# A hybrid decoder layer on one core: a third tile for the forms of x, later stores of the gated and merged blocks, a third fetched tile

## The chip, the cores and the metric

The kernel runs on one core of a Trainium2 chip, in one launch. The core has TensorE (matrix products; PE in the profile, with its weight loads as PEld), VectorE (DVE), ScalarE (ACT), GpSimd (POOL) and SyncE (SP). In this kernel SP issues most transfers between DRAM and the core's memory, GpSimd some, and both take them strictly in the order in which they are written. The metric is the device time of the core, in microseconds.

## The reference

The layer has 256 tokens and a width of 2048, in float32, with a tolerance that asks for more than single rounded products. Cut to what matters:

```python
h = _rmsnorm(x, pre_norm_g)
proj = jnp.einsum('bsd,de->bse', h, w_in)
(q_a, c_kv, k_rope, z_mla, c_in, b_gate, c_gate, z_conv,
 g_mla, g_conv) = jnp.split(proj, cuts, axis=-1)
...
attn = _causal_mla_attention(q_nope, q_rope, k_nope, k_rope, v)
attn = attn.reshape(b, s, MLA_WIDTH) * jax.nn.silu(z_mla)
y_mla = jnp.einsum('bse,ed->bsd', attn, w_o_mla)

u = c_gate * c_in
u_pad = jnp.pad(u, ((0, 0), (CONV_K - 1, 0), (0, 0)))
conv = sum(conv_w[k] * u_pad[:, k:k + s] for k in range(CONV_K))
y_conv = jnp.einsum('bse,ed->bsd', b_gate * conv * jax.nn.silu(z_conv), w_o_conv)

merged = jax.nn.sigmoid(g_mla) * y_mla + jax.nn.sigmoid(g_conv) * y_conv
out = jnp.einsum('bsd,de->bse', merged, w_out)
x = x + _rmsnorm(out, post_norm_g)
```

Latent attention (16 heads) and a short gated convolution run side by side on the normed input; each is projected back to 2048 channels, the two are weighted by sigmoid gates that are themselves products of the input, and one more projection follows.

## The kernel before

**Numbers in two parts.** Every float32 operand is split into a high and a low part of a narrower type, and TensorE forms three products (high by high, high by low, low by high). For a block of weights that arrived in a tile `raw`, ScalarE writes the high part `whi` and VectorE the low part `wlo` (`split_act`, L264 to L266). The weights of 1 MB each stream through three `raw` tiles, loaded by SP (L167): a load can go when VectorE has made the low part of the block three loads earlier, and when SP has got that far in its queue.

**Three stages.** The first, up to about 607 us, makes the attention's latents, heads and softmax and the channels of the convolution; its products are called `cv`, `z`, `qn`, `kn`, `sc` and others. The second, 607 to 965 us, makes the two sigmoid gates and the two projections back to 2048 channels. The third makes the output projection (`out`), the norm and the residual.

**Forms.** The gates are made by a scheme of fewer products: seven sums and differences of blocks of the input ("forms", named 11, 22, 12, 5, 6, 7 and 3) are prepared in the first stage, in four chunks. `make_forms` (L871) is a generator that is stepped beside the other work. Per chunk it loads the input into `x_area`, scales it, and makes for each form the high part on ScalarE (L902) and the low part on VectorE (L904, L906) in a tile `form`, of which there are two; SP stores it to `far_form` in DRAM (L909). So a form can be written only when the store of the form two earlier has landed. The sums 5, 6, 7 and 3 are made in four tiles `form_sum0` to `form_sum3`. A scheduler with a simulated timeline settles where the ScalarE and VectorE instructions of a form stand among those around them; transfers stay in program order.

**Sets and units.** In the second stage four sets s0 to s3 (`paired`, L1243) make the gates of one block c of 512 channels each; their weight sums come by loads into tiles `b` (L1251) and by transfers of GpSimd that add to what lies there (L1256). Between their steps stand units of plain products (`sq`): `at_both` by the attention's projection in s0 and s1, `cv_both` by the convolution's in s2 and s3; `turned_cv` loads bring the convolution's channels. The order is a list `seq` of units; a unit may have something put behind it by `later(n, fn)` (L1157), n units on, and the loads of weights are sorted in ahead of the units that need them.

**Gated and merged blocks.** A set has four gate tiles, a to d; the tile of `sd` in one set is that of `sa` in the next, and so on round. Each block of gate and projection, per c and per half t of the tokens, is multiplied in the gate's tile as soon as both are there. For the first branch `weigh` (L1216) does this, and `keep` has SP store the result in DRAM (L1148), one unit late. For the second branch `merge` (L1230) multiplies, adds the stored block, which GpSimd has fetched again (`fetch`, L1224, L1151) into one of two tiles `m`, transposes the sum into the gate's tile (L358) and has SP store it with four transfers to `far_m` (L366), one unit late; then it fetches the next. `turned_m` loads, two per pair of blocks and issued by GpSimd (L964), bring the transposed blocks back, and ScalarE and VectorE split them into `m_both` for the output products. `m_load[1]` is the loader of blocks 2 and 3; its first load was put behind the fourth unit of the last plain block, its second follows later.

Of the kernel before, what the change touches and what calls it, by code (L numbers as in the profile page):

```python
# [11 lines left out]
F32 = mybir.dt.float32  # L12
# [70 lines left out]
def tile_layer(ctx: ExitStack, tc: tile.TileContext, xw, w0, xb, x, pos, pvec, post_g, wc, wz, wcv, wkr, wqk, wqr, wv, cwr, wsq, xf, out):  # L83
# [210 lines left out]
    const.tile([P, LINE - 8 + 112 + P], F32, name="const_pad")  # L294
    cos_t = const.tile([P, S], F32, name="cos_t")
    sin_t = const.tile([P, S], F32, name="sin_t")
    r_x = const.tile([P, S], F32, name="r_x")
# [32 lines left out]
    qa = lp.tile([P, KR, 2 * S], F32R, name="qa")  # L330
    ckv = lp.tile([P, KR, 2 * S], F32R, name="ckv")
    kr = bp.tile([P, 2, S], F32R, name="kr")
    mask = bp.tile([P, 3 * P], F32, name="mask")
# [537 lines left out]
    def make_forms():  # L871

        kq = 2
        area = early_pool.tile([P, 2, kq, S], F32, name="x_area")
        sums_4 = [early_pool.tile([P, kq, P], F32, name=f"form_sum{i}") for i in range(4)]
        for c in range(KH // kq):
# [16 lines left out]
            a12, a22 = area[:, 1, :, :P], area[:, 1, :, P:]  # L893
            u, w, f7, f3 = (f[:, :, :] for f in sums_4)

# [3 lines left out]
            def part(n, src, sign=1.0):  # L899
                f = early_pool.tile([P, kq, 2, P], F32R, name=f"form{n}_{c}", tag="form", bufs=2)  # L900
                hi, lo = f[:, :, 0, :], f[:, :, 1, :]
                nc.scalar.activation(hi, src, AF.Copy, scale=sign)  # L902
                if sign == 1.0:
                    nc.vector.tensor_tensor(lo, src, hi.bitcast(F32), op=ALU.subtract)  # L904
                else:
                    nc.vector.scalar_tensor_tensor(lo, src, sign, hi.bitcast(F32), op0=ALU.mult, op1=ALU.subtract)  # L906
                w = kq * 2 * P
                return lambda: tc.keep_in_program_order(
                    nc.sync.dma_start(  # L909
                        out=far_form[n][:, c * w : (c + 1) * w], in_=f[:, :, :, :].rearrange("p k j c -> p (k j c)").bitcast(F32)  # L910
                    )
                )

            todo = (
                ("11", a11, 1.0, None), ("22", a22, 1.0, None), ("12", a12, 1.0, (u, a22, a21, ALU.subtract)),
                ("5", u, 1.0, (w, u, a11, ALU.add)), ("6", w, -1.0, (f7, a11, a21, ALU.subtract)),
                ("7", f7, 1.0, (f3, w, a12, ALU.subtract)), ("3", f3, 1.0, None),
            )
# [238 lines left out]
    def later(n, fn):  # L1157
        pending.setdefault(now[0] + n, []).append(fn)
# [57 lines left out]
    def weigh(nc_, t):  # L1216
        n, c = nc_
        g = gate_of[n, c, t]
        nc.vector.tensor_tensor(g[:, :], sums_of[n, c][t][:, :], g[:, :], op=ALU.mult)
        later(1, lambda: keep(("m", c, t), g))  # L1220

    fetched, wanted = {}, []

    def fetch():  # L1224
        if wanted:
            c, t = wanted.pop(0)
            fetched[c, t] = wide(f"m{c}_{t}", "y", 2)
            again(("m", c, t), fetched[c, t])

    def merge(nc_, t):  # L1230
# [5 lines left out]
        nc.vector.tensor_tensor(m[:, :], m[:, :], g[:, :], op=ALU.add)  # L1236
        go, _ = turned(m[:, :], g[:, :], 4, far_m[c][:, 512 * t : 512 * (t + 1)], nc.sync)
        later(1, go)
        later(1, fetch)
# [142 lines left out]

    for u, m in ((s3["V7"][1], 0), (v[3][3], 1)):
        also(u, m_load[m][0][0])
    also(s3["V4"][0], m_load[0][0][1])
    also(s3["V4"][1], m_load[0][1][1])

    def first_fetches(order):
        wanted.extend(order)
        fetch()  # L1390
        fetch()

# [66 lines left out]
    assert not wanted and not fetched  # L1459

    last_m = m_load[2][0]

# [199 lines left out]
```

## Time and profile before

| | |
|---|---|
| median of 3 runs | 1057.33 us |
| lowest, highest run | 1054.04, 1061.59 us |
| profiled execution | 1061.88 us |
| its span | 1059.6 us |
| TensorE, busy | 1019.5 us, 96% of the span |
| VectorE, busy | 803.5 us, 76% |
| ScalarE, busy | 591.8 us, 56% |
| GpSimd, busy | 167.8 us, 16% |
| mean transfer rate | 256 GB/s |
| mean granted clock of TensorE | 0.988 |

TensorE is the engine that sets the end: it runs almost without a break, so the place to look is each of its stops and what ended it. In a row of the timeline the first number is the start in us from the start of the span, the second the duration, and the bracket the idle time of that engine just before and what ended it. A row of the waits gives the total, how many times, and the longest. The granted clock is the share of full speed that TensorE was given; it is 1.00 nearly everywhere and 0.5 for some microseconds behind some of the stops.

### The profile page before, as it was taken

Reading aid. Unit: us, or ns where it says so; the run is one execution under the profiler, and the core shown is the slowest. Engines: PE = TensorE matmul, PEld = TensorE weight load, DVE = VectorE, ACT = ScalarE, POOL = GpSimd, SP = SyncE. Lnnn points to the kernel's source line nnn. Section 1 sums busy time; section 2 is a strip of 40 time slices with the busy share of each in tenths; the row PEclk is TensorE's granted clock in tenths of the full one; section 3 lists DMA queues with packets and bytes.
Section 4 is the critical chain, followed back from the end, with each engine's and each line's share of the span. In section 5 each row is a group of like instructions: output and inputs, shape, how many; then the busy total and the mean of one; then the engine's idle time right before and its main releaser. Section 6 shows DMA issues by size and latency. Waiting matters only on the chain.

```text
span 1059.6 us, 13048 instructions
## 1 busy us (share of the span) xinstructions
PE 1019.5 (96%) x4552; PEld 840.8 (79%) x4552; DVE 803.5 (76%) x1101; ACT 591.8 (56%) x854; POOL 167.8 (16%) x304
## 2 busy tenths in 40 slices
PE   9999999999999989999999987999998999899997
PEld 8887888887788878788888865888787788688886
DVE  7588878677797768766887696788787889586662
ACT  7666656555565555455564554564664664573551
POOL 4620421213211132112232220000000000100000
PEclk9999999999999999989999998999999999999999
DMA  9775877668775786847787899689679487956942
GB/s 368 272 236 225 288 245 262 219 205 286 228 279 203 211 271 240 293 168 240 235 298 282 307 319 373 262 302 261 236 255 355 159 292 187 284 210 242 366 186 79
DMA packets 58993, 271.02 MB, mean 256 GB/s; under 512 B 9104, under 2 KB 15888, under 8 KB 33584
## 3 DMA queue, kind: packets, MB, share of 16 engines
q1 hardware_dynamic: 45792, 226.94, 59.0%
q0 software_dynamic: 12848, 42.07, 15.0%
q10 hardware_dynamic: 288, 1.20, 0.3%
q8 instruction: 35, 0.57, 0.2%
q14 instruction: 30, 0.25, 0.1%
HBM read 241.88 MB, written 24.12 MB: 251 GB/s over the span
## 4 chain that ended last, share of the span: by engine, by line
PE 77%; DMA 11%; DVE 6%; ACT 3%; issue 1%; SPq 1%; DVEq 0%; ACTq 0%
PE cv L88 26%; PE sq L88 13%; PE out L88 8%; PE sX L88 7%; PE z L88 7%; DMA far_form<-form 6%; DMA raw<-wsq_dram 4%; PE sZ L88 3%; DVE wlo L266 2%; PE qa L88 2%; PE ckv L88 2%; PE sY L88 2%; ACT whi L265 2%; PE qn L88 1%; DMA x_area<-xf_dram 1%
## 5 line engine op out<-in xcount | busy, mean ns | idle before, releaser
L265 ACT ACTIVATE whi<-raw 128x1024 fp32r<-128x1024 f32 (+1 forms) x302 | 305.2, 1027 | 252.2 <-PE cv L88 86.1
L266 DVE TENSOR_TENSOR wlo<-raw,whi 128x1024 fp32r<-128x1024 f32 (+1 forms) x300 | 352.2, 1187 | 121.1 <-ACT whi L265 101.6
L88 PE MATMUL cv<-whi,x_both 128*128 128x512 f32 x1024 | 323.4, 392 | 8.1 <-ACT cv_f L811 4.9
L88 PEld LDWEIGHTS cv<-whi,x_both 128*128 128x128 f32 x1024 | 193.6, 189 | 50.6 <-ACT cv_f L811 6.2
L88 PE MATMUL cv<-wlo,x_both 128*128 128x512 f32 x512 | 200.6, 392 | 1.5 <-DVE wlo L266 1.5
L88 PEld LDWEIGHTS cv<-wlo,x_both 128*128 128x128 f32 x512 | 96.9, 189 | 21.2 <-DVE wlo L266 1.8
L266 DVE TENSOR_TENSOR slo_V<-b,shi_V 128x1024 fp32r<-128x1024 f32 x60 | 71.6, 1220 | 18.4 <-PE sq L88 11.7
L265 ACT ACTIVATE shi_V<-b 128x1024 fp32r<-128x1024 f32 x60 | 61.2, 1052 | 37.8 <-PE sq L88 26.9
L88 PE MATMUL z<-whi,x_both 128*128 128x512 f32 x256 | 79.9, 389 | 0.0
L88 PE MATMUL sq<-whi,cv_both 128*128 128x512 f32 x256 | 63.9, 404 | 7.7 <-ACT whi L265 7.7
L366 POOL DMA_DIRECT2D far<-via x64 | 35.4, 559 | 224.0 <-DVE via L358 222.5
L88 PE MATMUL sq<-whi,at_both 128*128 128x512 f32 x256 | 62.3, 396 | 7.8 <-ACT whi L265 7.8
L88 PEld LDWEIGHTS sq<-whi,cv_both 128*128 128x128 f32 x256 | 50.0, 197 | 19.3 <-ACT whi L265 8.7
L88 PEld LDWEIGHTS sq<-whi,at_both 128*128 128x128 f32 x256 | 48.9, 192 | 19.1 <-ACT whi L265 8.8
L88 PEld LDWEIGHTS z<-whi,x_both 128*128 128x128 f32 x256 | 48.1, 188 | 9.9
L88 PE MATMUL sX<-shi_V,form 128*128 128x512 f32 x192 | 47.8, 391 | 2.3 <-ACT sb L1300 2.3
L88 PE MATMUL z<-wlo,x_both 128*128 128x512 f32 x128 | 49.8, 389 | 0.0
L88 PE MATMUL out<-whi,m_both 128*128 128x512 f32 x208 | 49.4, 389 | 0.0
L88 PEld LDWEIGHTS out<-whi,m_both 128*128 128x128 f32 x208 | 39.0, 188 | 8.1
L88 PEld LDWEIGHTS sX<-shi_V,form 128*128 128x128 f32 x192 | 35.8, 188 | 10.9 <-ACT sb L1300 3.6
L1256 POOL DMA_DIRECT2D b<-wsq_dram x10 | 8.7, 894 | 186.1 <-ACT whi L265 125.1
L266 DVE TENSOR_TENSOR slo_Q<-b,shi_Q 128x1024 fp32r<-128x1024 f32 x28 | 33.4, 1220 | 4.7 <-PE sq L88 3.2
(301 smaller groups left out, 1560.4 us busy)
## 6 DMA issues: line engine op xcount, KB each, us to landing
raw<-wcv_dram SPq DMA_DIRECT2D x64, 1024.0 KB, 6.1
raw<-wsq_dram SPq DMA_DIRECT2D x48, 1024.0 KB, 6.8
b<-wsq_dram SPq DMA_DIRECT2D x26, 1024.0 KB, 5.2
raw<-wz_dram SPq DMA_DIRECT2D x16, 1024.0 KB, 4.8
b<-wsq_dram POOLq DMA_DIRECT2D x10, 1024.0 KB, 10.7
raw<-wqk_dram SPq DMA_DIRECT2D x8, 1024.0 KB, 7.7
far_form<-form SPq DMA_DIRECT2D x28, 256.0 KB, 7.7
form<-far_form SPq DMA_DIRECT2D x7, 1024.0 KB, 11.2
```

What stands on the lines that cost most here:

```text
L88: return tc.keep_in_program_order(nc.tensor.matmul(*a, **kw))
L265: a = nc.scalar.activation(hi, src, AF.Copy)
L266: b = nc.vector.tensor_tensor(lo, src, hi.bitcast(F32), op=ALU.subtract)
L366: tc.keep_in_program_order(queue.dma_start(out=f[i], in_=m))
L1256: tc.keep_in_program_order(nc.gpsimd.dma_start(out=dst[:, :], in_=wsq[n, c + b, k], accum_op=ALU.add))
```

## The change

Five things change. The forms have three tiles in place of two, and the sums 7 and 3 are written over those of 5 and 6, so two tiles of sums are gone; the rotary tables `cos_t` and `sin_t` move to another pool. `weigh` stores its gated block four units late, not one. `merge` stores the merged blocks of c = 0 and 1 four units late on SP, and those of c = 2 and 3 at once on GpSimd. There are three tiles `m` for fetched blocks, and up to three fetches are made at first. The first load of `m_load[1]` is issued behind the whole list of units.

```diff
--- before.py
+++ after.py
@@ -292,8 +292,6 @@
     for _ in range(8):
         matmul(idle[:, :P], one, one, start=True, stop=True)
     const.tile([P, LINE - 8 + 112 + P], F32, name="const_pad")
-    cos_t = const.tile([P, S], F32, name="cos_t")
-    sin_t = const.tile([P, S], F32, name="sin_t")
     r_x = const.tile([P, S], F32, name="r_x")
     r_both = const.tile([P, LINE], F32, name="r_both")
     nc.gpsimd.memset(r_both[:, :], 0.0)
@@ -329,6 +327,8 @@
     lp = lstack.enter_context(tc.tile_pool(name="lp", bufs=1, side="right"))
     qa = lp.tile([P, KR, 2 * S], F32R, name="qa")
     ckv = lp.tile([P, KR, 2 * S], F32R, name="ckv")
+    cos_t = bp.tile([P, S], F32, name="cos_t")
+    sin_t = bp.tile([P, S], F32, name="sin_t")
     kr = bp.tile([P, 2, S], F32R, name="kr")
     mask = bp.tile([P, 3 * P], F32, name="mask")
     nc.gpsimd.memset(mask[:, :], 0.0)
@@ -872,7 +872,7 @@
 
         kq = 2
         area = early_pool.tile([P, 2, kq, S], F32, name="x_area")
-        sums_4 = [early_pool.tile([P, kq, P], F32, name=f"form_sum{i}") for i in range(4)]
+        sums_2 = [early_pool.tile([P, kq, P], F32, name=f"form_sum{i}") for i in range(2)]
         for c in range(KH // kq):
             for i in range(2):
                 tc.keep_in_program_order(
@@ -891,13 +891,13 @@
             yield
             a11, a21 = area[:, 0, :, :P], area[:, 0, :, P:]
             a12, a22 = area[:, 1, :, :P], area[:, 1, :, P:]
-            u, w, f7, f3 = (f[:, :, :] for f in sums_4)
+            u, w = (f[:, :, :] for f in sums_2)
 
             def tt(o, a, b, op):
                 nc.vector.tensor_tensor(o, a, b, op=op)
 
             def part(n, src, sign=1.0):
-                f = early_pool.tile([P, kq, 2, P], F32R, name=f"form{n}_{c}", tag="form", bufs=2)
+                f = early_pool.tile([P, kq, 2, P], F32R, name=f"form{n}_{c}", tag="form", bufs=3)
                 hi, lo = f[:, :, 0, :], f[:, :, 1, :]
                 nc.scalar.activation(hi, src, AF.Copy, scale=sign)
                 if sign == 1.0:
@@ -913,8 +913,8 @@
 
             todo = (
                 ("11", a11, 1.0, None), ("22", a22, 1.0, None), ("12", a12, 1.0, (u, a22, a21, ALU.subtract)),
-                ("5", u, 1.0, (w, u, a11, ALU.add)), ("6", w, -1.0, (f7, a11, a21, ALU.subtract)),
-                ("7", f7, 1.0, (f3, w, a12, ALU.subtract)), ("3", f3, 1.0, None),
+                ("5", u, 1.0, (w, u, a11, ALU.add)), ("6", w, -1.0, (u, a11, a21, ALU.subtract)),
+                ("7", u, 1.0, (w, w, a12, ALU.subtract)), ("3", w, 1.0, None),
             )
             for n, src, sign, following in todo:
                 go = part(n, src, sign)
@@ -1217,14 +1217,14 @@
         n, c = nc_
         g = gate_of[n, c, t]
         nc.vector.tensor_tensor(g[:, :], sums_of[n, c][t][:, :], g[:, :], op=ALU.mult)
-        later(1, lambda: keep(("m", c, t), g))
+        later(4, lambda: keep(("m", c, t), g))
 
     fetched, wanted = {}, []
 
     def fetch():
         if wanted:
             c, t = wanted.pop(0)
-            fetched[c, t] = wide(f"m{c}_{t}", "y", 2)
+            fetched[c, t] = wide(f"m{c}_{t}", "y", 3)
             again(("m", c, t), fetched[c, t])
 
     def merge(nc_, t):
@@ -1234,8 +1234,8 @@
         g, m = gate_of[n, c, t], fetched.pop((c, t))
         nc.vector.tensor_tensor(g[:, :], sums_of[n, c][t][:, :], g[:, :], op=ALU.mult)
         nc.vector.tensor_tensor(m[:, :], m[:, :], g[:, :], op=ALU.add)
-        go, _ = turned(m[:, :], g[:, :], 4, far_m[c][:, 512 * t : 512 * (t + 1)], nc.sync)
-        later(1, go)
+        go, _ = turned(m[:, :], g[:, :], 4, far_m[c][:, 512 * t : 512 * (t + 1)], nc.gpsimd if c > 1 else nc.sync)
+        later(0 if c > 1 else 4, go)
         later(1, fetch)
 
     sums_of, gate_of = {}, {}
@@ -1380,15 +1380,14 @@
         old = u[3]
         u[3] = lambda: (old and old(), fn())
 
-    for u, m in ((s3["V7"][1], 0), (v[3][3], 1)):
-        also(u, m_load[m][0][0])
+    also(s3["V7"][1], m_load[0][0][0])
     also(s3["V4"][0], m_load[0][0][1])
     also(s3["V4"][1], m_load[0][1][1])
 
     def first_fetches(order):
         wanted.extend(order)
-        fetch()
-        fetch()
+        for _ in range(min(3, len(order))):
+            fetch()
 
     also(s2["V6"][1], lambda: first_fetches([(0, 1), (0, 0), (1, 0), (1, 1)]))
     also(s3["V6"][1], lambda: first_fetches([(2, 1), (2, 0)]))
@@ -1458,6 +1457,7 @@
 
     assert not wanted and not fetched
 
+    m_load[1][0][0]()
     last_m = m_load[2][0]
 
     def out_products(pss, w, kk, ts=range(NT)):
```

TensorE's order is the same in both kernels. In the other engines' queues these places matter below.

ScalarE, second chunk of the forms (`form5_1` is form 5 of chunk 1; `half` is a copy for a rope, `cv_f` an eviction of a product of the channels, `whi` a weight's high part). Before:

```order
L433 ACTIVATE half_2443<-qr3_2416 128x256 [waits PE_49]
L902 ACTIVATE form5_1_2602<-form_sum0_1014 128x2x128 [waits DMAHW1_49]
L811 ACTIVATE cv_f_112<-cv4_0_2277,r_both_99 128x512 [waits PE_49]
L265 ACTIVATE whi51_1024_2530<-raw51_2458 128x1024 [waits DVE_49,PE_49]
L265 ACTIVATE qr_2437<-f_2442 64x256 [waits DVE_49]
```

After:

```order
L433 ACTIVATE half_2441<-qr3_2414 128x256 [waits PE_49]
L902 ACTIVATE form6_1_2639<-form_sum1_1015 128x2x128 [waits DMAHW1_49]
L811 ACTIVATE cv_f_110<-cv4_0_2275,r_both_97 128x512 [waits PE_49]
L265 ACTIVATE whi51_1024_2528<-raw51_2456 128x1024 [waits DVE_49,PE_49]
L265 ACTIVATE qr_2435<-f_2440 64x256 [waits DVE_49]
```

At the same place stands the next form, 6 in place of 5, and it waits for the same transfer semaphore; every form of a chunk from the third on has moved up by one form's place in this way.

ScalarE, the end of the same chunk (`kn` is the high part of a head's key, `qn_hi` of its query). Before:

```order
L433 ACTIVATE half_2723<-kn3_1_2699 128x256 [waits PE_49,Activation_49]
L902 ACTIVATE form3_1_2895<-form_sum3_1017 128x2x128 [waits DMAHW1_49]
L265 ACTIVATE kn_2677<-f_2716 128x256 [waits DVE_49]
L265 ACTIVATE kn_2677<-f_2722 128x256 [waits DVE_49]
L265 ACTIVATE whi56_1024_2818<-raw56_2728 128x1024 [waits PE_49]
```

After:

```order
L265 ACTIVATE qn_hi_2673<-f_2690 128x256 [waits DVE_49]
L433 ACTIVATE half_2721<-kn3_1_2697 128x256 [waits PE_49,Activation_49]
L265 ACTIVATE kn_2675<-f_2714 128x256 [waits DVE_49]
L265 ACTIVATE kn_2675<-f_2720 128x256 [waits DVE_49]
L265 ACTIVATE whi56_1024_2816<-raw56_2726 128x1024 [waits PE_49]
```

Form 3, the last of the chunk, no longer stands ahead of `kn`; it has taken the place of form 7 earlier on.

SP, the transition from set s2 to s3 (`b` are loads of weights for the gates, `raw` the streamed weights, `far_m` the stores of merged blocks of `sd`, `sa`, `sb`, `sc`, four transfers each). Before:

```order
L1251 DMA b_1_0_7561<-wsq_dram 128x2048
L366 DMA far_m_648<-sd_7556 32x4x128 x4
L1251 DMA b_1_1_7601<-wsq_dram 128x2048
L167 DMA raw_7624<-wsq_dram 128x2048
L1251 DMA b_1_2_7626<-wsq_dram 128x2048
L1251 DMA b_1_3_7649<-wsq_dram 128x2048
L366 DMA far_m_648<-sa_7086 32x4x128 x4
L366 DMA far_m_649<-sb_7344 32x4x128 x4
L366 DMA far_m_649<-sc_7394 32x4x128 x4
L167 DMA raw_7728<-wsq_dram 128x2048
L167 DMA raw_7752<-wsq_dram 128x2048
```

After:

```order
L1251 DMA b_1_0_7561<-wsq_dram 128x2048
L1251 DMA b_1_1_7597<-wsq_dram 128x2048
L167 DMA raw_7620<-wsq_dram 128x2048
L1251 DMA b_1_2_7622<-wsq_dram 128x2048
L1251 DMA b_1_3_7645<-wsq_dram 128x2048
L366 DMA far_m_648<-sd_7556 32x4x128 x4
L167 DMA raw_7714<-wsq_dram 128x2048
L167 DMA raw_7738<-wsq_dram 128x2048
L366 DMA far_m_648<-sa_7078 32x4x128 x4
L366 DMA far_m_649<-sb_7342 32x4x128 x4
L366 DMA far_m_649<-sc_7394 32x4x128 x4
L167 DMA raw_7843<-wsq_dram 128x2048
```

The stores of `sd` have moved behind three loads of `b` and one of `raw`, and two loads of `raw` now stand ahead of the twelve stores of `sa`, `sb` and `sc`, where they stood behind them. In the transition from s1 to s2 both `turned_cv` loads, which stood behind the stores of gated blocks `sa`, `sb` and `sc`, likewise stand ahead of them, with a `raw` and two `b` loads in between.

## Prediction

> **What bounds the kernel now.** I read the page first, for the busy shares.
>
> ```profile
> span 1059.6 us, 13048 instructions
> PE 1019.5 (96%) x4552; PEld 840.8 (79%) x4552; DVE 803.5 (76%) x1101; ACT 591.8 (56%) x854; POOL 167.8 (16%) x304
> ```
>
> TensorE is busy for all but 40 us, and the change takes no product away. What can be won is a part of those 40 us, and the half-clock stretches behind some of its stops. So next I read TensorE's timeline at its stops that this change can reach (the bracket is the idle time and what ended it); the last row is an undisturbed run of 16 products.
>
> ```profile
> 95.30 0.50 PE L88 MATMUL cv<-wlo,x_both 128*128 128x512 f32 x1 [1.51 <-DVE wlo L266]
> 250.56 0.50 PE L88 MATMUL cv<-whi,x_both 128*128 128x512 f32 x1 [1.77 <-ACT cv_f L811]
> 280.46 0.39 PE L88 MATMUL sc<-kn,qn_hi 128*128 128x256 f32 x1 [1.70 <-DVE kn L266]
> 388.78 0.50 PE L88 MATMUL cv<-whi,x_both 128*128 128x512 f32 x1 [1.59 <-ACT cv_f L811]
> 393.38 0.50 PE L88 MATMUL cv<-whi,x_both 128*128 128x512 f32 x1 [1.57 <-ACT cv_f L811]
> 451.22 0.80 PE L88 MATMUL cv<-whi,x_both 128*128 128x512 f32 x1 [3.13 <-ACT cv_w L815]
> 817.99 5.54 PE L88 MATMUL sq<-whi,cv_both 128*128 128x512 f32 x16 [3.35 <-ACT whi L265]
> 907.93 5.36 PE L88 MATMUL sq<-whi,cv_both 128*128 128x512 f32 x16 [4.35 <-ACT whi L265]
> 954.09 3.79 PE L88 MATMUL sq<-whi,cv_both 128*128 128x512 f32 x16
> ```
>
> The six early stops fall where the forms are made; the waits of ScalarE and its timeline say why.
>
> ```profile
> ACT form L902 <- DMA far_form<-form: 40.8, 15, 5.7
> 249.51 0.42 ACT L902 ACTIVATE form<-form_sum 128x256 fp32r<-128x256 f32 x1 [5.75 <-DMA far_form<-form]
> 277.88 0.42 ACT L902 ACTIVATE form<-form_sum 128x256 fp32r<-128x256 f32 x1 [3.28 <-DMA far_form<-form]
> 387.74 0.42 ACT L902 ACTIVATE form<-form_sum 128x256 fp32r<-128x256 f32 x1 [5.57 <-DMA far_form<-form]
> 449.30 0.42 ACT L902 ACTIVATE form<-x_area 128x256 fp32r<-128x256 f32 x1 [4.18 <-DMA far_form<-form]
> ```
>
> ScalarE stands 40.8 us in all until an earlier form's store has landed and its tile is free; what stands behind it (`cv_f`, `kn`, `cv_w`) then comes late to TensorE. The two late stops (817.99, 907.93) wait for weights instead, and each costs more than its gap: the 16 products behind it take 5.54 and 5.36 us where 3.79 is normal, 1.75 and 1.57 more, since the granted clock falls.
>
> **Forms.** The obvious reading is that a third tile takes the waits away. The order of the two kernels says otherwise: ScalarE's forms all move up by one place. The form that now stands at 249.51 (fifth of its chunk, `cv_f` behind it as before) is the next one, and with three tiles it needs the same store, on the same semaphore; SP issues that store at the same place between the same weights. So the waits at 249.51, 387.74 and 449.30 stay where they are, with the stops of 1.77, 1.59 and 3.13 behind them. What goes is the last wait of each chunk. At 277.88 no form stands ahead of `kn<-f` any more: the stop of 1.70 goes. What stands behind it can move up by as much as the 3.28 us that ScalarE stood there, against a stop of 1.70. At 391.8 the DVE's order matters:
>
> ```profile
> 388.19 0.43 DVE L904 TENSOR_TENSOR form<-form_sum,form 128x256 fp32r<-128x256 f32 x1 [4.78 <-ACT form L902]
> 391.31 0.42 DVE L512 TENSOR_TENSOR f<-rp_a,rp_b 128x256 f32<-128x256 f32 x1
> ```
>
> The low part of the form stood 4.78 us at DVE's head with the ropes behind it; `f` came at 391.73, and behind `f` on ScalarE the second `cv_f`. In the changed order the ropes stand ahead of it and `f` can move up by 4.78, against a stop of 1.57: it goes, unless ScalarE, which still stands until 387.74, is the next to be late there. In the first chunk DVE has one such operation fewer ahead of the low weights at 95.30: 0.4 of 1.51. The sums written in place add nothing, and each operation that is moved on costs 0.43 of DVE beside work that has no stop behind it. Sum: 1.70 + 1.57 + 0.4 = 3.7, between 2 (one of the two stops stays) and 4.
>
> **Gated blocks stored four units late.** The queue of SP in front of the stop at 814.6:
>
> ```profile
> SPq L1148 <- DVE sa L1219: 9.2, 1, 9.2
> 790.19 1.93 SPq L964 DMA_DIRECT2D turned_cv<-far_cv  x2
> 796.51 0.33 SPq L167 DMA_DIRECT2D raw<-wsq_dram  x1
> turned_cv<-far_cv SPq DMA_DIRECT2D x2, 512.0 KB, 8.8
> 816.88 2.00 ACT L265 ACTIVATE whi<-raw 128x1024 fp32r<-128x1024 f32 x2 [7.33 <-DMA raw<-wsq_dram]
> 778.00:790.00 12.00, 12.00 (x55) 9.94 (x53) 11.28 (x12) 7.73 (x9) 0.87 (x1) 1.00 0.63 208
> 804.00:817.00 13.00, 10.64 (x47) 8.47 (x46) 8.08 (x5) 2.13 (x3) 0.00 (x0) 1.00 1.00 396
> 812.00:824.00 12.00, 8.65 (x31) 6.61 (x30) 10.35 (x7) 6.21 (x7) 0.00 (x0) 0.86 0.88 354
> ```
>
> (The last two figures of a stretch are the DMA share and GB/s; the one ahead of them the granted clock.) SP stood 9.2 us for the gated block `sa`, and both `turned_cv` loads behind it. The weights that TensorE lacks are issued at 796.51, when their buffer comes free, and take 20 us through a full pipe. In the new order the `turned_cv` loads stand ahead of the three stores and can go up to those 9.2 us earlier, into a stretch where the pipe is 0.63 full: 2 x 512 KB less in front of those weights, 2.6 to 3.0 us at 396 to 354 GB/s. The three stores stay in front of them, and a third fetch of 256 KB comes in, 0.7 us. The weights land 2.2 us earlier, the stop shrinks from 3.35 to 1.15, and I take it that the clock then holds (the stops of 1.5 to 1.8 us above have single products of 0.39 and 0.50 behind them, no slow run): 2.2 + 1.75 = 4.0, between 0 (the pipe decides alone) and 5.1 (all of it).
>
> The Trainium skill, "TensorE: Matmul & The Clock Gate", section "What's actually happening", has the array fall to half rate after an idle window of about 3.4 us that runs freely; by it the 3.35-us stop would as a rule cost no clock, and this term would be 2.2, not 4.0. The trace disagrees: clock 0.86 in the stretch behind it.
>
> In the first pair of sets the stores of `sd`, `sb`, `sc` also move behind three loads. The eviction `sa<-sX` reuses the tile of `sd`, so ScalarE may now stand there, with a split of `b` behind it:
>
> ```profile
> 702.34 0.44 SPq L1251 DMA_DIRECT2D b<-wsq_dram  x1
> 712.98 2.04 ACT L265 ACTIVATE shi_V<-b 128x1024 fp32r<-128x1024 f32 x2 [1.52 <-PE sq L88]
> kept_m<-sb SPq DMA_DIRECT2D x1, 256.0 KB, 8.7
> ```
>
> The third of these loads goes at 702.34 and the store of `sd` behind it; with the 8.7 us of a store in a full pipe it lands near 711.5, when the eviction has ended in the trace of before, at 711.5 too (712.98 less 1.52). ScalarE stands idle for 1.52 us just behind it. I take 0; if the store came several us later still, the price is a stop like the one at 907.93, 5.9.
>
> **Merged blocks.** SP in front of the stop at 903.6:
>
> ```profile
> 883.15 2.35 DVE L266 TENSOR_TENSOR wlo<-raw,whi 128x1024 fp32r<-128x1024 f32 x2
> 886.15 1.78 SPq L366 DMA_DIRECT2D far_m<-sa  x4
> 899.92 0.63 SPq L167 DMA_DIRECT2D raw<-wsq_dram  x1
> 906.82 2.00 ACT L265 ACTIVATE whi<-raw 128x1024 fp32r<-128x1024 f32 x2 [12.11 <-DMA raw<-wsq_dram]
> ```
>
> Here the queue itself is the cause: the buffer is free by 885.5, but the load stands behind twelve stores that wait for transposes, until 899.92. In the changed order two loads stand ahead of them. Alone the load took 6.9 us; sharing the pipe evenly with the accumulating transfers it takes twice that and is there at 899.3, where 902.5 is needed. Stop and slow clock go: 4.35 + 1.57 = 5.9, and at least half of it if the pipe is fuller than that. GpSimd's fetch no longer waits for `sa` either.
>
> **The last two blocks and the third fetch.** GpSimd now issues these 16 stores at once, and the load of `turned_m` for c = 2 stands behind all of them:
>
> ```profile
> L366 POOL DMA_DIRECT2D far<-via x64 | 35.4, 559 | 224.0 <-DVE via L358 222.5
> 967.20 0.55 POOL L964 DMA_DIRECT2D turned_m<-far_m  x1 [36.27 <-DVE wlo L266]
> 970.76 0.71 DVE L358 STREAM_TRANSPOSE sc<-m_area 128x512 f32<-128x512 f32 x1
> 972.35 1.16 ACT L265 ACTIVATE m_both<-turned_m 128x512 fp32r<-128x512 f32 x2 [3.41 <-DMA turned_m<-far_m]
> 986.73 3.79 PE L88 MATMUL out<-whi,m_both 128*128 128x512 f32 x16
> ```
>
> A store costs GpSimd 0.56 us. After the transpose (971.47) four of them are out at 973.7, and the load goes at about 974.3 instead of 967.20. It took 5.1 us; so it lands at 979.4, and with 2.3 us of splitting (1.16 on ScalarE and as much on DVE) it is ready at 981.7, 5.0 us ahead of its use at 986.73. Cost nothing; the cover is gone if it lands 5 us later, and less if ScalarE holds a weight split ahead of it. SP's weights lose eight stores in front of them, behind which nothing stops today. The moved rotary tables and the third fetched tile cost only space.
>
> **The sum.** 3.7 + 4.0 + 5.9 = 13.6, between 5 and 15. The profiled execution took 1061.88 us, 2.28 more than its span, and 4.55 more than the median of the runs (1057.33). How much of these 4.55 is stops that go I can't see; I give half, 2.3. So 1061.88 - 2.3 - 13.6 = **1046.0**, and for none or all of it 1043.7 to 1048.3. This kernel's runs can tell about 1% from no change: below 1046.8 is faster, above 1067.9 slower.
>
> **Rivals.** *The form waits go altogether* (0.12): for it speaks the plain count of tiles, against it the unchanged places and semaphores. 1.77 + 1.59 + 3.13 more, and 0.43 of 6.8 us, 2.9, of slow clock behind the last of them:
>
> ```profile
> 451.20:458.00 6.80, 6.78 (x18) 5.36 (x19) 5.62 (x14) 4.96 (x11) 0.00 (x0) 0.57 0.20 56
> ```
>
> That is 9.4 less, 1036.6. *The pipe decides at 814* (0.20): for it speaks 1.00 of DMA share from 804 to 817; the 4.0 stay and 1050.0 remains. *Only the forms' part arrives* (0.08), because the earlier weights at 885 make the accumulating transfers late, the next thing that TensorE waits for: 1055.9. *The end turns against it* (0.08), slower: if full transfers and not the queue set the landings, both late stops stay, and at the end the load of c = 2 takes not 5.1 but 16.6 us, as GpSimd's fetches did around 790:
>
> ```profile
> m<-kept_m POOLq DMA_DIRECT2D x2, 256.0 KB, 16.6
> ```
>
> Then it is ready at 993.2, 6.5 late, with 1.6 of slow clock. The stores of c = 3, by the same measure, land near 990 and its load near 1007; split by 1009, it is 3.3 late for a use two units of 5.4 us after that of c = 2 (997.6, moved to 1005.7 by the 8.1), with 1.6 of slow clock again. 13.0 lost against 3.7 won: 1068.9. It decides from 5 us of lateness on. Against it: the same load took 5.1 us with SP's loads beside it.
>
> The Trainium skill, "DMA: Bandwidth & Descriptors", section "Issuing engines are not separate DMA queues", says that transfers started by any engine share the same 16 engines, so that another issuer saves only issue time. It speaks against a gain from GpSimd's stores; my sum has none there, and no run here shows it yet.
>
> **Chances.** My forecast has 0.50, 0.30 of it under 1046.8; 0.02 is for what I don't see, half each way. Faster: 0.30 + 0.12 + 0.01 = 0.43; slower: 0.06 of the last rival and 0.01; same: 0.50. The range 1037 to 1057 leaves out the slower rival and half of the first.
>
> **What would show it.** ScalarE's wait for `far_form` should fall from 40.8 only to some 30, with stops left near 249, 387 and 448 and none at 279 and 392; the stop at 903 gone, the one at 814 under 2 us with a clock of 1.00 behind it; the load of `turned_m` for c = 2 landing before 984. I am wrong if 249, 387 and 448 go too, or if a new stop over 3 us stands at 710, 880 or 986.

## The result: 0.87% less, two of the three terms as forecast

Over 20 runs each the changed kernel took 1050.31 us in the median, the kernel before 1058.15; the ratio is 0.9913 with a 95% interval of 0.989 to 0.9936, that is 9.2 us less (6.8 to 11.6). The measured median lies inside the forecast range of 1037 to 1057; the forecast itself was 1046.0, or 11.3 less than the median then known (1057.33). The interval leaves out no change, but 0.87% is under the 1% that the prediction asked for "faster".

From the page of the changed kernel: TensorE stands for 32 us now (1049.8 less 1017.3), not 40.

```profile
span 1049.8 us, 13040 instructions
PE 1017.3 (97%) x4552; PEld 840.1 (80%) x4552; DVE 802.1 (76%) x1101; ACT 592.2 (56%) x854; POOL 175.7 (17%) x320
```

Its stops, in TensorE's timeline of the changed kernel; the last row is the run of products that stood behind the 4.35 us before. (Here and below, a `sq<-whi` row with fewer than 16 products is cut off by the window that was read; its duration is not that of the whole run.)

```profile
94.93 0.50 PE L88 MATMUL cv<-wlo,x_both 128*128 128x512 f32 x1 [0.86 <-DVE wlo L266]
249.11 0.50 PE L88 MATMUL cv<-whi,x_both 128*128 128x512 f32 x1 [0.85 <-ACT cv_f L811]
384.59 0.50 PE L88 MATMUL cv<-whi,x_both 128*128 128x512 f32 x1 [0.93 <-ACT cv_f L811]
416.62 0.58 PE L88 MATMUL sc<-kn,qn_hi 128*128 128x256 f32 x1 [3.81 <-DVE kn L266]
448.56 0.50 PE L88 MATMUL cv<-whi,x_both 128*128 128x512 f32 x1 [1.93 <-ACT cv_w L815]
808.03 1.65 PE L88 MATMUL sq<-wlo,cv_both 128*128 128x512 f32 x6 [0.83 <-DVE wlo L266]
813.05 1.22 PE L88 MATMUL sq<-whi,cv_both 128*128 128x512 f32 x2 [3.37 <-ACT whi L265]
899.67 3.79 PE L88 MATMUL sq<-whi,cv_both 128*128 128x512 f32 x16
```

The stops of 1.70 and 1.57 near 279 and 392 are gone, and so is the one near 903 with its slow clock. Those near 249, 387 and 448 are there, shorter. The one near 814 has not shrunk: 3.37, with a new one of 0.83 ahead of it. And near 413 stands a longer one, of 3.81, where ScalarE waits for the input of the next chunk with a head's key behind it. ScalarE's waits and its forms in the changed kernel:

```profile
ACT form L902 <- DMA far_form<-form: 30.5, 12, 5.0
ACT x_area L888 <- DMA x_area<-xf_dram: 8.5, 5, 4.6
248.07 0.42 ACT L902 ACTIVATE form<-form_sum 128x256 fp32r<-128x256 f32 x1 [4.83 <-DMA far_form<-form]
383.54 0.42 ACT L902 ACTIVATE form<-form_sum 128x256 fp32r<-128x256 f32 x1 [4.91 <-DMA far_form<-form]
446.64 0.42 ACT L902 ACTIVATE form<-form_sum 128x256 fp32r<-128x256 f32 x1 [2.98 <-DMA far_form<-form]
```

The wait for the stores fell from 40.8 to 30.5 us: most of it has stayed with three tiles. The queue of SP at the two late places, in the changed kernel:

```profile
790.79 1.22 SPq L1148 DMA_DIRECT2D kept_m<-sa  x1
792.05 0.62 SPq L1148 DMA_DIRECT2D kept_m<-sb  x1
792.72 0.50 SPq L1148 DMA_DIRECT2D kept_m<-sc  x1
793.32 0.92 SPq L167 DMA_DIRECT2D raw<-wsq_dram  x2
...
880.64 3.82 SPq L167 DMA_DIRECT2D raw<-wsq_dram  x2
884.51 1.99 SPq L366 DMA_DIRECT2D far_m<-sa  x4
```

At 880.64 the two loads go ahead of the stores `sa`, `sb` and `sc`, and the stop is gone. At 793.32 the load goes right behind three stores that cost SP 2.3 us.

TensorE's products stand in the same order in every kernel here, so the time between two given products can be compared stage by stage. This table is worked out from the traces; each figure is how many us longer (or, with a minus, shorter) the stage took than in the profile of the kernel before. Stages are named by the times of that profile; one execution each.

```
                             0-600   600-800  800-825  825-880  880-925  925-end
the whole change             -5.8     -0.3     +2.3      0.0     -6.1      0.0
the same, another execution -10.1     -1.2     +1.2      0.0     -6.1      0.0
forms alone                  -9.1     -2.1     -1.5      0.0     +0.9      0.0
gated blocks alone           -4.2     -2.6     +1.0     +0.1     +1.2      0.0
merged blocks alone          -4.8     -0.9     -1.6     +0.1     -6.1     +0.2
last two blocks undone       -6.1     -1.0     +1.2     -0.1     -6.1      0.0
third fetched tile undone    -9.2     -1.8     +0.7     -0.1     -6.1     +0.6
gated blocks five late       -5.8     -0.1     -2.2     +0.1     -6.1      0.0
turned_cv splits in order    -9.1     +0.8     +1.2     +0.1     -6.1      0.0
two tiles, forms in order   -11.0     +1.0     +1.3     +0.1     +0.4      0.0
forms in order              -10.0     -1.9     +1.2     -0.1     -6.1      0.0
three edits together        -14.8     -0.3     -3.3     +0.1     -6.1      0.0
and x_area in order         -17.8     +0.5     -1.5      0.0     -6.1      0.0
```

Two things are to be seen before any experiment is told. From 880 us on the change does one thing, 6.1 us in every kernel with the merged blocks moved. And the first stage differs by several us between executions of the same code: the rows "gated blocks alone" and "merged blocks alone" have the first stage of the kernel before and are 4.2 and 4.8 us shorter there. For that stage the timed ratios decide, not one profile.

### The profile page after: what moved, and what is told of

It is laid out like the page before. It is cut to its first block, busy times and chain, and to the rows that moved or that the text cites. A ratio compares the mean times of both kernels' runs of the same rounds, so it can differ in the third digit from the quotient of the medians.

```text
span 1049.8 us, 13040 instructions
## 1 busy us (share of the span) xinstructions
PE 1017.3 (97%) x4552; PEld 840.1 (80%) x4552; DVE 802.1 (76%) x1101; ACT 592.2 (56%) x854; POOL 175.7 (17%) x320
## 4 chain that ended last, share of the span: by engine, by line
PE 74%; DMA 11%; DVE 6%; issue 4%; ACT 3%; POOL 1%; SPq 1%; DVEq 0%; ACTq 0%; POOLq 0%
PE cv L88 23%; PE sq L88 14%; PE out L88 8%; PE sX L88 7%; PE z L88 6%; DMA far_form<-form 4%; DMA raw<-wsq_dram 3%; PE sZ L88 3%; DVE wlo L266 2%; PE qa L88 2%; PE sY L88 2%; DMA cw<-cwr_dram 2%; PE ckv L88 2%; PE qn L88 1%; DMA x_area<-xf_dram 1%
## 5 line engine op out<-in xcount | busy, mean ns | idle before, releaser
L88 PEld LDWEIGHTS sq<-whi,at_both 128*128 128x128 f32 x256 | 49.2, 193 | 18.1 <-ACT whi L265 7.8
```

Of the source, the lines that this page charges most:

```text
L88: return tc.keep_in_program_order(nc.tensor.matmul(*a, **kw))
```

## The experiments

**The parts, each alone.** The forms' part alone (three tiles, two sums in place, the rotary tables moved):

```diff
-f = early_pool.tile([P, kq, 2, P], F32R, name=f"form{n}_{c}", tag="form", bufs=2)
+f = early_pool.tile([P, kq, 2, P], F32R, name=f"form{n}_{c}", tag="form", bufs=3)
```

> Only the forms' part of the change (three tiles, two sums written in place, rotary tables moved). My theory: ScalarE's wait for far_form falls from 40.8 to about 30 us, the stops near 279 and 392 go, those near 249, 387 and 448 stay, and the run gains 3.7 to 5 us (ratio 0.995 to 0.9965); the stops at 814 and 903 keep their 3.4 and 4.4 us, since all that leads to them moves up with TensorE. Rival (given back): the landing of the late weights is fixed by the pipe of transfers; then what the forms win comes back as longer stops at 814 and 903 (7 us and more) and the gain is under 1 us. Rival (the waits vanish): gain 9 us or more.

Ratio 0.996 (0.9932 to 0.9988), 4.2 us. The wait for the stores is 31.4 us in this execution. Over all the profiles here it is 29.3 to 34.5 us in 11 to 13 waits with three tiles at the scheduler's places (seven executions), and 40.8, 33.3 and 38.0 us in 15, 15 and 17 waits with two (the kernel before and the two that follow). So some waits go and most stay: the first theory holds. The single stops are a weaker sign than the waits: those near 279 and 392 stand in none of the seven executions, but with two tiles they stand in two of three, and are absent from "gated blocks alone", where the first stage is that of the kernel before. Giving back falls: the stop near 814 is 3.49 us, about as long as the 3.35 before, although TensorE is 11 us ahead when it gets there (803.5 against 814.6); the weights' loads move up with it.

```profile
807.00 3.94 PE L88 MATMUL sq<-whi,cv_both 128*128 128x512 f32 x16 [3.49 <-ACT whi L265]
807.00:814.00 7.00, 7.00 (x31) 5.70 (x32) 7.00 (x7) 5.94 (x7) 0.00 (x0) 1.00 0.69 268
```

Note the clock in the second row (the first of the last three figures): 1.00. The same stop, and no slow run behind it.

The gated blocks' stores alone:

```diff
-later(1, lambda: keep(("m", c, t), g))
+later(4, lambda: keep(("m", c, t), g))
```

> Only the gated blocks' stores four units late. In the profile of the whole change the stop near 814 stayed at 3.4 us with a second one of 0.8 ahead of it. Theory A (SP's queue): the weights go only behind the three moved stores, which SP now issues just ahead of them in 2.3 us; that eats the 1 MB that left the pipe. Then the stop is here again 3 to 4.5 us and the time is that of the kernel before within 2 us (ratio 0.998 to 1.002). Theory B (given back): the loads came as forecast, but TensorE came sooner because of the forms; then here, without the forms' gain, the stop is under 1.2 us and the run gains 2 to 4 us (0.996 to 0.998).

Ratio 1.0003 (0.998 to 1.0025): nothing. At the place, TensorE's timeline of this kernel shows two stops, 4.1 us together against 3.35:

```profile
807.95 1.65 PE L88 MATMUL sq<-wlo,cv_both 128*128 128x512 f32 x6 [1.38 <-DVE wlo L266]
812.32 3.91 PE L88 MATMUL sq<-whi,cv_both 128*128 128x512 f32 x9 [2.72 <-ACT whi L265]
```

Theory A fits. In this execution the first stage came out 4.2 us shorter without the forms' part, so it does not by itself rule out that TensorE had come sooner; the forms alone do, where TensorE was 11 us ahead and the stop hardly longer. At the place the part rather cost something: in the table's column 800-825 the seven executions with stores four units late stand at +0.7 to +2.3, the four with stores one unit late at 0, -1.5, -1.6 and +1.3. Half clock followed the stop in all of the seven and in two of the four. This is the term that failed.

The merged blocks' stores of c = 0 and 1 alone:

```diff
-later(1, go)
+later(1 if c > 1 else 4, go)
```

> Only the merged blocks of c = 0 and 1 stored four units late, on SP; all else as before. Theory: the stop of 4.35 us at 903.6 goes and the slow clock behind it too: 5 to 6 us less (ratio 0.9943 to 0.9953), about all that the second half of the change wins. Rival: the stop goes only together with the third fetched tile or the gated stores, which free GpSimd's queue for the accumulating transfers; then a stop of over 2 us stays near 903 and the gain is under 3 us.

Ratio 0.9923 (0.99 to 0.9945), 8.1 us with 5.8 to 10.6 by the interval, where 5 to 6 were expected; 6.1 at the place itself by the table, and no stop near 903 in its profile. Neither the third fetched tile nor the gated stores are needed for it.

The last two blocks put back on SP, one unit late, and the `turned_m` load at its old place, the rest as changed:

```diff
-go, _ = turned(m[:, :], g[:, :], 4, far_m[c][:, 512 * t : 512 * (t + 1)], nc.gpsimd if c > 1 else nc.sync)
-later(0 if c > 1 else 4, go)
+go, _ = turned(m[:, :], g[:, :], 4, far_m[c][:, 512 * t : 512 * (t + 1)], nc.sync)
+later(1 if c > 1 else 4, go)
```

> The whole change, but with the last two blocks' stores on SP one unit late and the turned load of c = 2 at its old place. Theory: GpSimd's stores and the later load are covered and cost and win nothing: the ratio to the kernel before is that of the whole change, 0.991 within 0.002. Rival: the eight stores that stood in front of SP's weights near 970 cost something once the rest is faster; then this run is 2 us or more slower than the whole change (0.993 and above), with a stop between 965 and 985.

Ratio 0.9899 (0.9871 to 0.9926), within the interval of the whole change; from 925 us to the end both take the same time to 0.01 us. GpSimd's part wins nothing and costs nothing.

**Why the gated part won nothing.** There are two suspects. One is SP's three stores, straight ahead of the load in the rows above. The other is the order on VectorE and ScalarE, where the `cv_both` splits have moved ahead of the weights' low parts. VectorE before (first two rows) and after:

```profile
793.00 3.49 DVE L266 TENSOR_TENSOR wlo<-raw,whi 128x1024 fp32r<-128x1024 f32 x3
802.71 1.29 DVE L266 TENSOR_TENSOR cv_both<-turned_cv,cv_both 128x512 fp32r<-128x512 f32 x2
...
789.25 1.29 DVE L266 TENSOR_TENSOR cv_both<-turned_cv,cv_both 128x512 fp32r<-128x512 f32 x2
790.46 2.36 DVE L266 TENSOR_TENSOR wlo<-raw,whi 128x1024 fp32r<-128x1024 f32 x2
```

There is one experiment for each. The stores one unit later, so that the load is ahead of them:

```diff
-later(4, lambda: keep(("m", c, t), g))
+later(5, lambda: keep(("m", c, t), g))
```

> The whole change with the gated blocks stored five units late instead of four: at the transition s1 to s2 the load of the missing weights then stands ahead of the three stores of sa, sb, sc (0.75 MB), not behind them; ScalarE's and VectorE's order there stays. Theory S (stores in front): the weights land 2 us or more earlier from their issue (16.5 us instead of 18.5), the stop of 3.4 us near 809 falls to 1.5 or less, the one of 0.8 ahead of it stays, and the run is 2 to 5 us faster than the whole change (0.987 to 0.989 of the kernel before). Theory V (VectorE frees the buffer late) alone: the load still goes late, and only what the stores took of the pipe is won: stop 1.3 to 3. Theory P (the pipe whatever the order): stop 3.0 to 3.8 as before, ratio 0.991.

SP's and TensorE's timelines of this kernel:

```profile
791.05 1.05 SPq L167 DMA_DIRECT2D raw<-wsq_dram  x1
...
808.29 1.66 PE L88 MATMUL sq<-wlo,cv_both 128*128 128x512 f32 x6 [0.94 <-DVE wlo L266]
811.51 3.95 PE L88 MATMUL sq<-whi,cv_both 128*128 128x512 f32 x16 [1.56 <-ACT whi L265]
```

The load goes at 791.05, 18.9 us ahead of the moment at which TensorE stands for it (811.51 less 1.56 is 809.95); in the whole change it was 16.4 (793.32 to 809.68). The stop falls from 3.37 to 1.56, and the stage takes 4.5 and 3.4 us less than in the two profiles of the whole change, slow clock included. Ratio 0.9883 (0.9845 to 0.9921); in time this cannot be told from the whole change, so it is the place that decides. The buffer had been free: what held the load was SP, busy with three stores. From its issue to TensorE's use the load took no less, 20.5 us against 19.7 (813.05 less 793.32), against what the expectation said; it is the issue that moved.

The splits of the second `turned_cv` tile in program order, behind the low parts again:

```diff
-def go(keep=False):
+def go(keep=both.name == "cv" and first == 2):
```

> The whole change with the splits of the second turned_cv tile kept in program order, so that they stand again behind the low parts of the weights on VectorE and ScalarE, as in the kernel before; SP's queue as in the change. Theory V (VectorE): the cv_both splits that moved ahead (four of 0.65 us) let the buffer of the missing weights come free 2.4 us later against TensorE; without them the load goes 2.4 us earlier, the stops near 807 and 809 (0.8 + 3.4) fall to under 2 together, ratio 0.987 to 0.989. Theory S (the stores in front) or P (the pipe): the load's landing does not follow its issue, 3 us and more stay, ratio 0.990 to 0.992.

The stop of 0.83 is gone; the other stays.

```profile
809.85 2.50 PE L88 MATMUL sq<-whi,cv_both 128*128 128x512 f32 x5 [3.35 <-ACT whi L265]
```

Ratio 0.991 (0.9876 to 0.9944), no gain that can be told. So the order on VectorE made the small stop (in the whole change an addition of `b` waited there for its transfer, with a `wlo` behind it) and not the large one; this theory was wrong on the main point.

**The third fetched tile.** Two tiles and two first fetches, the rest as changed:

```diff
-fetched[c, t] = wide(f"m{c}_{t}", "y", 3)
+fetched[c, t] = wide(f"m{c}_{t}", "y", 2)
```

> The whole change with two tiles for fetched blocks and two fetches at first, as before. Theory: the third fetch puts 0.25 MB into the full pipe ahead of the weights near 809; without it they land about 0.7 us earlier (stop 2.5 to 3 in place of 3.4), and nothing else moves: ratio 0.990 to 0.992, within noise of the whole change. Rival: the third tile is what frees GpSimd's queue near 876 and so part of the 6 us won at 903; then a stop comes back between 880 and 925.

```profile
807.69 4.81 PE L88 MATMUL sq<-whi,cv_both 128*128 128x512 f32 x13 [2.71 <-ACT whi L265]
```

2.71 in place of 3.37 (3.35 to 3.39 in the five executions with the third fetch and the stores four units late): this agrees with the prediction's estimate of 0.7 us for 256 KB in the full pipe. Near 903 nothing comes back. Ratio 0.9892 (0.9854 to 0.9929), in time no difference that can be told.

**Tile or place.** The forms' waits were forecast to stay because the scheduler pulled each form up by as much as the new tile gave. If that is so, the high parts held in program order should find their tile free:

```diff
-nc.scalar.activation(hi, src, AF.Copy, scale=sign)
+tc.keep_in_program_order(nc.scalar.activation(hi, src, AF.Copy, scale=sign))
```

> The whole change with the high parts of the forms kept in program order on ScalarE, which puts nearly all of them one or more places later than the scheduler's simulated times do; three tiles. Theory: the waits for far_form were kept by the scheduler, which pulled each form up by as much as the third tile gave; placed later they find their tile free: ScalarE's wait falls from 30 to under 10 us, the stops near 248, 383 and 446 go, and the run gains 3 to 6 us more (ratio 0.985 to 0.988). Rival: the stores, now later in SP's queue, stop the loads behind them, or the loads of x_area for the next chunk come later; then new stops stand between 200 and 470 and the ratio is 0.991 or worse.

In this kernel no wait for `far_form` is left among ScalarE's waits, and the stops near 94, 248, 383 and 446 are gone. Ratio 0.9872 (0.9841 to 0.9902). A stop of 1.09 stands near 304; one of 0.8 to 0.9 stood there in two executions with the scheduler's places. The stop at the chunk's input stays, 2.91 in this execution:

```profile
413.19 0.58 PE L88 MATMUL sc<-kn,qn_hi 128*128 128x256 f32 x1 [2.91 <-DVE kn L266]
```

The same one line in the kernel before, with its two tiles:

> The kernel before, with two form tiles and four tiles of sums, and only the forms' high parts kept in program order on ScalarE. Theory T (tile and place together): at the same places two tiles make each form wait for a store that is one younger; some waits stay (ScalarE's wait for far_form 10 to 25 us, where three tiles at these places showed none), the gain over the kernel before is 3 to 7 us (ratio 0.9935 to 0.997). Rival (place alone): the third tile is not needed once the scheduler no longer pulls the forms up; wait under 5 us and the gain in the first stage is that of the pinned form of the change, 8 to 10 us (ratio 0.991 to 0.9925).

ScalarE's wait in this kernel:

```profile
ACT form L902 <- DMA far_form<-form: 3.0, 3, 1.4
```

3.0 us of 40.8, with no third tile. Ratio 0.9935 (0.9911 to 0.996): 6.9 us (4.2 to 9.4), against 4.2 (1.3 to 7.2) for the third tile. The wait speaks for the rival (place alone); the time lies at the upper end of what the theory gave. In the first stage of the table this kernel is as short as the one with three tiles (-11.0 and -10.0), one execution each. For the waits the place was the matter, and the tile a small part of it; in time the two intervals overlap, so that the place won more than the tile is likely and not shown.

**Together.** The load ahead of the stores, the splits and the forms in order:

> All three together: gated blocks five units late, the second turned_cv tile's splits and the forms' high parts in program order. If the three theories hold and add up: the two stops near 807 gone or under 0.5, form waits under 10, ratio 0.981 to 0.985. If they share one limit (the pipe of transfers), the gains do not add: 0.986 or more.

Ratio 0.9845 (0.9808 to 0.9881), 1042.43 us in the median. This fits gains that add, but the interval also reaches the 0.986 of the rival. No wait for `far_form` is left; of the two late stops one of 1.59 us remains near 800, where under 0.5 was expected. With the scaling of the chunk's input in program order too, so that no key stands behind its load:

```diff
-nc.scalar.activation(x, x, AF.Copy, scale=col("pre_g", KH * i + kq * c + k))
+tc.keep_in_program_order(nc.scalar.activation(x, x, AF.Copy, scale=col("pre_g", KH * i + kq * c + k)))
```

> The best so far (gated blocks five units late, the second turned_cv tile's splits and the forms' high parts in program order) with the scaling of x_area in program order too. Theory: the stop near 410 (0.9 to 3.8 us in all runs so far), where ScalarE stands for the x_area load with a head's key behind it, goes, and the run gains 1 to 3 us more than the best: ratio 0.982 to 0.9845. Rival: the forms then come later by as much, and their stores stop SP's loads: no gain or a loss, 0.985 or more.

Ratio 0.9773 (0.9736 to 0.9809), 1034.26 us: 24 us below the kernel before and the fastest here, better than was expected of it. From 1 us up to 595 us its TensorE has no stop of 0.35 us or more. Why it gained some 8 us on the kernel without this edit, and not 1 to 3, is open: the two profiled executions have nearly the same span (1035.6 and 1035.3). What the runs show is less spread: 1033.3 to 1037.3 us here, 1037.0 to 1045.8 without the edit, 1050.7 to 1065.3 for the kernel before. What is left:

```profile
PE 1013.5 (98%) x4552; PEld 838.3 (81%) x4552; DVE 801.6 (77%) x1101; ACT 591.7 (57%) x854; POOL 175.9 (17%) x320
...
799.17 5.54 PE L88 MATMUL sq<-whi,cv_both 128*128 128x512 f32 x16 [1.85 <-ACT whi L265]
```

**The change once more.**

> The whole change as it is, once more beside the others: ratio 0.991 within 0.002; its stop near 809 again 3.4 us with 0.8 to 1.0 ahead of it and the one near 903 absent. What differs from its first profile between 200 and 470 us is what one execution differs from another by; I expect up to 5 us there and under 0.5 us from 825 us on.

Ratio 0.9901 (0.9864 to 0.9939). From 825 us on the two profiles of the change agree within 0.01 us; in the first stage they differ by 4.4 us, and the stop near 413 that was 3.81 is 0.41.

## Why the prediction was right or wrong, point by point

- **Forms, 3.7: right in mechanism, and in size as far as can be told.** 4.2 (1.3 to 7.2). Most waits stayed where the order had them, and 15 to 17 of them became 11 to 13; program order without the tile takes away more of them than the tile with the scheduler's places. The rival by which the waits vanish is refuted for this change. That the sum of three single stops came so near is in part luck, since these stops differ from execution to execution. What the step did not see is ScalarE's stand for the chunk's input ahead of `kn`: 1.24 us in the profile of before, 4.63 in that of the change (a stop of 3.81), and 0.41 of stop in its second one. The tile did not make it: "gated blocks alone", with the first stage of the kernel before, has a stop of 2.58 there.
- **Gated blocks, 4.0: wrong.** Measured: 0.3 more, between 2.1 less and 2.6 more. The step that failed is "the three stores stay in front of them": it priced them as bytes that were in the pipe already, and gave SP's time to issue them no cost. Before, SP issued them at 787 to 790, while the load's buffer was still in use, in 0.33 us each (first three rows; the last two are the landing of the weights, as ScalarE sees it, before and after). Now SP issues them when the buffer is free and the pipe fuller (a DMA share of 0.91 from 790 to 794, where it was 0.54 from 786 to 790 before), and they take 1.22, 0.62 and 0.50 us. The load so goes 1.8 us nearer to its use (18.1 us ahead of it before, 16.4 now), which is what its landing won (20.3 us before, 18.5 now). The 0.7 of the third fetch was right. The 1.75 for a clock that holds did not come either: half clock followed, for 6.8 us in the first profile of the change and 3.4 in the second. The new 0.83 from VectorE's order was not foreseen at all, though the changed place of the `cv_both` splits stood in the order.

```profile
787.45 0.33 SPq L1148 DMA_DIRECT2D kept_m<-sa  x1
788.04 0.33 SPq L1148 DMA_DIRECT2D kept_m<-sb  x1
789.78 0.32 SPq L1148 DMA_DIRECT2D kept_m<-sc  x1
...
816.88 2.00 ACT L265 ACTIVATE whi<-raw 128x1024 fp32r<-128x1024 f32 x2 [7.33 <-DMA raw<-wsq_dram]
811.95 2.00 ACT L265 ACTIVATE whi<-raw 128x1024 fp32r<-128x1024 f32 x2 [9.90 <-DMA raw<-wsq_dram]
```

- **Merged blocks, 5.9: right.** 6.1 at the place in every run with this part; 8.1 (5.8 to 10.6) in time. The load took 10.8 us in the change, less than the 13.8 that the prediction allowed for.
- **The first pair of sets, 0: right in time, by less cover than the text had it.** ScalarE does stand for the store of `sd`, 8.2 us in the profile of the change, with a stop of 0.39 on TensorE behind it; in its second one it stands 0.9 us, and no stop follows.

```profile
712.38 0.60 ACT L1300 ACTIVATE sa<-sX 128x512 f32<-128x512 f32 x1 [8.18 <-DMA kept_m<-sd]
```

- **The last two blocks, 0: right.** The load of c = 2 goes behind GpSimd's stores and its splitting begins 4.6 us ahead of the use; 7.3 was forecast, since the load took longer than 5.1 us.

```profile
963.83 0.56 POOL L964 DMA_DIRECT2D turned_m<-far_m  x1
972.27 1.15 ACT L265 ACTIVATE m_both<-turned_m 128x512 fp32r<-128x512 f32 x2 [1.32 <-DMA turned_m<-far_m]
976.90 3.79 PE L88 MATMUL out<-whi,m_both 128*128 128x512 f32 x16
```

- **The sum.** 13.6 less the failed 4.0 is 9.6, counted from the profiled execution; from the median then known, with the 2.3 taken off, it is 7.3. The medians differ by 9.2, and the three parts alone add to 12.0 (4.2, -0.3 and 8.1); these agree within their intervals. How near the total came is therefore in part luck. The result is nearly the rival "the pipe decides at 814" (1050.0), in time, but not in its reason: the full pipe alone did not decide, since one unit's shift of three stores in SP's queue took 1.8 us of the stop away.

## What to carry to other kernels

Another buffer helps in full only if the instruction that waits for it stays where it was: look in the new order whether a scheduler has pulled it up by as much as the buffer gave, and try the place before the memory. When transfers move in an in-order queue, price the time that the queue takes to issue them at the new place, in the state in which the pipe is there, and not their bytes alone; put the load that an engine will stand for ahead of stores that nobody waits for yet. One profile is enough for a stop that repeats to 0.01 us and not for a stage that differs by 4 us between executions of the same code.

## What the runs showed of the hardware that was not expected

A stop's length did not settle whether the slow clock follows. The same stop near 814 had 5.54 us for its 16 products behind 3.35 us, and none of that behind 3.49 (3.94 us, clock 1.00, the rows of the forms alone) or behind 3.33 in the kernel with the merged blocks alone:

```profile
812.29 3.95 PE L88 MATMUL sq<-whi,cv_both 128*128 128x512 f32 x16 [3.33 <-ACT whi L265]
```

while 1.85 us in the last kernel above was enough for 5.54, and in the profile of the whole change the clock was down for longer than before:

```profile
811.00:819.00 8.00, 5.95 (x14) 4.69 (x15) 5.77 (x5) 5.26 (x6) 0.00 (x0) 0.57 0.82 325
```

The kernel before had a case too, which the prediction passed over: eight products in 3.94 us, the time of sixteen at full speed, behind 1.90 us.

```profile
620.64 3.94 PE L88 MATMUL sq<-wlo,at_both 128*128 128x512 f32 x8 [1.90 <-DVE wlo L266]
```

What tells these cases apart is where the idle time lies. In each of the fourteen traces the granted clock changes only at whole multiples of 3.41 us from its first change. From 10 us on these multiples cut each trace into stretches, and the idle time of TensorE in each can be counted. Of the stretches at full speed, 46 held 1.84 us or more of it, and half speed followed each of them; 4085 held under 1.65 us, and it followed none; of the 15 in between it followed 5. After a stretch at half speed another followed where 0.64 us or more were idle (23 of 23) and none where it was 0.53 or less (0 of 51). The 3.33 us above fall into two stretches, 1.52 and 1.81 us (the length less TensorE's busy time, the two figures at the start of the first two rows), and the clock holds. The 1.85 us of the last kernel fall into one (last two rows).

```profile
807.07:810.48 3.41, 1.89 (x9) 1.23 (x7) 3.26 (x2) 0.00 (x0) 0.00 (x0) 1.00 1.01 425
810.48:813.90 3.42, 1.61 (x7) 1.25 (x8) 2.18 (x3) 2.72 (x3) 0.00 (x0) 1.00 1.00 424
813.90:817.30 3.40, 3.40 (x17) 2.81 (x16) 3.40 (x4) 3.40 (x5) 0.00 (x0) 1.00 0.60 190
...
796.47:799.88 3.41, 1.56 (x7) 0.99 (x6) 3.23 (x3) 1.82 (x2) 0.00 (x0) 1.00 1.10 415
799.88:803.29 3.41, 3.41 (x10) 2.58 (x9) 3.41 (x4) 3.02 (x4) 0.00 (x0) 0.50 0.97 341
```

The Trainium skill, "TensorE: Matmul & The Clock Gate", section "What's actually happening", has a window of about 3.4 us that runs freely, and half rate after at least one idle window. The length and the free running agree with these traces; a whole idle window as the condition does not, since about 1.8 of 3.41 us were enough. For a sum it means, as an estimate from these counts: a stop alone under some 1.6 us costs no clock, one over some 3.7 us always does, and between the two the clock is a chance, not 1.75 us that go with the stop.
